# Compressed-branch logits: keys held in the array and queries streamed, instead of queries held and keys streamed

## Chip, cores and metric

One core of one Trainium2 chip runs one program. The metric is the time of one execution on the device in microseconds (us). The kernel is a float32 kernel: products that need the accuracy are made from a high and a low part of each operand, each part in a 4-byte format that TensorE streams in one pass (`F32R` in the code).

## The reference, cut to what matters

Two layers of a decoder trunk on 512 tokens of 1024 channels. Layer 0 mixes tokens with a short convolution, layer 1 with sparse attention; each layer has a half-step SwiGLU feed-forward before and after its mixer. The change touches one of the attention's three branches, the compressed one. 16 heads stand in 4 groups of 4, the head dimension is 64, and each group has 31 compressed keys:

```python
dist_c = t[:, None] - cmp_end[None, :]
s_c = (jnp.einsum('bghqd,bgnd->bghqn', qb, k_cmp).astype(f32) * scale
       + rb[:, :, t5_bucket(dist_c)])
p_c = masked_softmax(s_c, dist_c >= 0)
o_c = jnp.einsum('bghqn,bgnd->bghqd', p_c.astype(v_cmp.dtype), v_cmp)
```

The selected and the window branch (`o_s`, `o_w`) are ordinary causal attention over 512 keys here, since all 8 blocks of 64 tokens are selected, and `out` is the sum of the three branches, each times a gate.

## The kernel before, in words

The program runs feed-forward, convolution, feed-forward, feed-forward, attention, feed-forward one after the other. A scheduler orders the instructions of each engine when the program is built, by their order in the source, by priorities and by a model of durations; on the chip each engine then takes its own list strictly in that order and waits at an instruction until what it needs is there.

The attention's inner part is `attend`. Its loop over `v` runs through 32 units `(g, q, b)`: group, head in the group, branch (0 and 1 are the two branches over 512 keys). At a step it makes the logits of unit `v + 3` on TensorE (`s`, L1061), adds the bias table `tb` and takes the extremum on VectorE (L1071), takes exponentials on ScalarE (L1080), scales them on GpSimd (`L`, L1091), turns those of unit `v + 1` by transposes (`pt`, L1100, then `pth` on ScalarE and `ptl` on VectorE), and applies those of unit `v` to the values (`o`, L1117 and L1118). Other work is put between: projections of the next group's queries (`nat`), turning of queries and keys (`pq` and `pk` in `turners`), the output projection of a finished group (`y`, then `yt` on ScalarE and an addition to `x` on GpSimd), and loads of weights (`wraw`, `whi`, `wlo`, `ehhi`, `ehlo`).

`compressed(g)` is the compressed branch of one group, cut by `yield` into pieces that the loop runs at steps `8g - 2`, `8g - 1` (two) and `8g`. For group 0 these stand at the start of the loop. The logits go into one PSUM tile `pc` (tag `nat`): columns are query block `i` (4), head `q` (4) and key `n` (32 with the pad). `Q[q]` holds a head's 512 queries in 128 rows: the high part in one half of the rows and the low part in the other. `kch` and `kcl` hold the keys' high and low parts, repeated in both halves, so two products per tile give all four part products. After that VectorE adds the bias (`lc`, L1022), takes the minimum (`mc`) and subtracts (`pcs`), ScalarE takes exponentials, VectorE normalises, four transposes (`pct`, L1041) turn the weights, and `finish` applies them with `vz` to the sum `o` of a head.

PSUM has four tags of two tiles each: `nat`, `s`, `t`, `o`. The tag `nat` serves the projections `nat`, the turned keys and queries, `pc`, `pct` and `y`; an instruction that starts a tile waits until the readers of the tile that had the place before are done. The SBUF tag `sq` has two tiles as well and serves the squares of a projection and `yt`.

Of the kernel before, what the change touches and what calls it, by code (L numbers as in the profile page):

```python
# [13 lines left out]
F32 = mybir.dt.float32  # L14
F32R = mybir.dt.float32r
I32 = mybir.dt.int32
AF = mybir.ActivationFunctionType
# [5 lines left out]
P = 128  # L23
# [10 lines left out]
HD = 64  # L34
NHEAD = 16
NG = 4
NCMP = 31
NPAD = 32
# [15 lines left out]
def decoder_kernel(ctx, tc, xT, cT, ng, adaw, adab, ffi, ffo, cwi, cw, cwo,  # L54
                   nwi, nwg, pos, w1, w2, qg, kg, nwo, rb, onehot, rowok, out):
    nc = tc.nc

    def pool(es, name, bufs, **kw):
        kw.setdefault("reuse_waits", "tile")
        return es.enter_context(tc.tile_pool(name=name, bufs=bufs, **kw))  # L60
# [16 lines left out]
    def psum(name, tag="mm"):  # L77
        tag = next(six) if tag == "mm" else {"pr": "o"}.get(tag, tag)
        return ps.tile([P, T], F32, name=name, tag=tag, bufs=2)
# [4 lines left out]
    def tmp(name, n=T, tag="t"):  # L84
        bufs, size = TAGS[tag]
        return tp.tile([P, n], F32, name=name, tag=tag, padded_shape=[P, size], bufs=bufs)
# [3 lines left out]
    ap = ada_es.enter_context(tc.tile_pool(name="ada", bufs=4))  # L90
# [13 lines left out]
    ident = cst.tile([P, P], F32, name="ident")  # L104
# [64 lines left out]
    def split(src, hi, lo):  # L169
        nc.scalar.activation(hi, src, AF.Copy)  # L170
        nc.vector.tensor_tensor(lo, src, hi, ALU.subtract)  # L171
# [535 lines left out]
    def nsa(s, nrm, nxt, w0, ahead):  # L707
        with ExitStack() as es:
# [112 lines left out]
            with ExitStack() as es2:  # L821
# [31 lines left out]
                run(v1[1:])  # L853
                keys(0, 1)
            return attend(es, s, nxt, ahead, K, Q, keys, heads, vn, kch, kcl, vcc, gsb, query_steps, value_steps, last_weight, hpool)


# [126 lines left out]
    def attend(nsa_es, s, nxt, ahead, K, Q, keys, heads, vn, kch, kcl, vcc, gsb, query_steps, value_steps, last_weight, hpool):  # L984
# [3 lines left out]
        with ExitStack() as es:  # L988
            at = pool(es, "at", 1)
# [3 lines left out]
            pcs = at.tile([P, NB, NG, NPAD], F32, name="pcs")  # L993
            vz = at.tile([P, NG, P], F32R, name="vz")
            nc.gpsimd.memset(vz.bitcast(F32), 0.0)

            def table(g, q):
                n = g * NG + q
                for e in range(P // NR):
                    src = bass.AP(tensor=tbl.tensor, offset=tbl.offset + n * NR * TBL + P - 1 - NR * e,  # L1000
                                  ap=[[TBL - 1, NR], [1, T]])
                    nc.sync.dma_start(tb[NR * e:NR * (e + 1), q, :], src)
# [4 lines left out]
            fl = lambda a: a.rearrange("p i q n -> p (i q) n")  # L1007

            def compressed(g):
                pc = psum("pc", "nat")  # L1010
                gc = slice(g * NPAD, (g + 1) * NPAD)
                for i in range(NB):
                    for q in range(NG):
                        oc = pc[:, (i * NG + q) * NPAD:(i * NG + q + 1) * NPAD]
                        for n, m in enumerate((kch, kcl)):
                            nc.tensor.matmul(oc, Q[q][:, i * P:(i + 1) * P], m[:, gc], start=(n == 0), stop=(n == 1))
                    if i == 1:
                        yield
                pv = pc.rearrange("p (i q n) -> p i q n", i=NB, q=NG)
                for i in range(NB):  # L1020
                    nb, c0 = 8 * i + 7, 415 - 128 * i
                    nc.vector.tensor_tensor(lc[:, i, :, 0:nb], pv[:, i, :, 0:nb],  # L1022
                                            tb[:, :, c0:c0 + 16 * (nb - 1) + 1:16], ALU.add)
                mc = sp.tile([P, 16], F32, name="mc", bufs=2)
                nc.vector.tensor_reduce(mc, fl(lc), axis=AX.X, op=ALU.min)
                nc.vector.tensor_tensor(fl(pcs), fl(lc), mc[:, :, None].to_broadcast([P, 16, NPAD]), ALU.subtract)
                nc.scalar.activation(pcs, pcs, AF.Exp, scale=-1.0)
                yield
                sc = sp.tile([P, 16], F32, name="sc", bufs=2)
                nc.vector.tensor_reduce(sc, fl(pcs)[:, :, 0:NCMP], axis=AX.X, op=ALU.add)  # L1030
                fc = sp.tile([P, NB, NG], F32, name="fc", bufs=2)
                nc.vector.reciprocal(fc.rearrange("p i q -> p (i q)"), sc)
                gv = gsb[:, :, g * 12:(g + 1) * 12].rearrange("p i (q r) -> p i q r", r=3)
                nc.vector.tensor_tensor(fc, fc, gv[:, :, :, 0], ALU.mult)
                nc.vector.tensor_scalar(fc[:, 0, :], fc[:, 0, :], rowm, None, op0=ALU.mult)
                nc.vector.tensor_tensor(fl(pcs), fl(pcs), fc.rearrange("p i q -> p (i q)")[:, :, None].to_broadcast([P, 16, NPAD]),
                                        ALU.mult)
                yield
                pt = psum("pct", "nat")
                for i in range(NB):  # L1040
                    nc.tensor.transpose(pt[:, i * P:(i + 1) * P], pcs[:, i].rearrange("p q n -> p (q n)"), ident)  # L1041
                split(pt, pch, pcl)
                for q in range(NG):
                    nc.gpsimd.tensor_copy(vz[q * NPAD:q * NPAD + NCMP, q, :],
                                          vcc[g * NPAD:g * NPAD + NCMP].rearrange("p a b -> p (a b)"))
                yield
# [113 lines left out]
            for g in range(NG):  # L1160
                v0 = 8 * g
                c = compressed(g)
                for q in range(NG):
                    tables[max(v0 - 9 + 2 * q, START)].append((g, q))
                if g:
                    needed[v0 - 5].append(lambda g=g: heads(g, 0))
                    needed[v0 - 4].append(lambda g=g: keys(g, 0))
                    needed[v0 - 3].append(lambda g=g: keys(g, 1))
                    needed[v0 - 2].append(lambda g=g: heads(g, 1))
                for v in (v0 - 2, v0 - 1, v0 - 1, v0):  # L1170
                    needed[v].append(lambda c=c: next(c))
# [7 lines left out]
            def share(v):  # L1179
                for steps, v0, v1 in shares:  # L1180
                    if v0 <= v < v1:
                        n = 11
                        return steps, n * (v - v0 + 1) // (v1 - v0) - n * (v - v0) // (v1 - v0), v == v1 - 1
                return None, 0, False

            for v in range(START, N):
                a, b, u = v + LEAD, v + 1, v
                steps, n, end = share(v)
# [150 lines left out]
```

## Time and profile before

| | |
|---|---|
| three runs | 1966.22, 1966.75, 1969.36 us (median 1966.75) |
| the profiled execution | 1965.66 us, of which the profile's span is 1963.9 us |
| TensorE matmuls (PE) busy | 1914.6 us in 12680 matmuls |
| VectorE (DVE), ScalarE (ACT), GpSimd (POOL) busy | 1455.6, 879.6, 208.7 us |
| granted TensorE clock, mean over the span | 0.995 |
| the loop of `attend` | about 1364.5 to 1600 us of the span |

In rows of the timeline the columns are start in us, time in us, engine, line, operation, `output<-inputs`, the stationary operand's rows*columns and the shape that is streamed, and how often; in square brackets the idle time before it and what ended it. Matmuls overlap in the pipeline, so their cost is read from start to start. In a row of stretches each engine has its busy time and its number of instructions, then come the granted clock (PEclk), the share of the DMA engines and their GB/s. In rows of groups the busy time and the mean duration in ns stand behind the count.

### The profile page before, as it was taken

To read this page: it belongs to the slowest core of one execution; us is meant where nothing else is said; L and a number is where in the kernel's file an instruction comes from. 1 tells how busy PE (TensorE), PEld (TensorE's weight loads), DVE (VectorE), ACT (ScalarE), POOL (GpSimd) and SP (SyncE) were. 2 spreads that over 40 slices of the span, in tenths; PEclk is the share of its full clock that TensorE was granted. 3 is DMA by queue.
4 is the path that set the end of the run, shared out by engine and by line. 5 is a ranking of instruction groups with operands and counts; after the bars stand their busy time and mean duration, and the time that the engine had idled before them with its cause. 6 is when DMAs were issued, how large, how long until landed. Compare 5 with 4: busy or idle time off the path is not lost.

```text
span 1963.9 us, 32479 instructions
## 1 busy us (share of the span) xinstructions
PE 1914.6 (97%) x12680; PEld 1741.9 (89%) x12680; DVE 1455.6 (74%) x2557; ACT 879.6 (45%) x1417; POOL 208.7 (11%) x292
## 2 busy tenths in 40 slices
PE   5999999999999999999999999999999899999999
PEld 3878888898899898999989899999889789898989
DVE  7888889674467586878858687885786878686865
ACT  3322222242236353434635343466787956353532
POOL 0000000100010000000000000002444630010000
PEclk9999999999999999999999999999999999999999
DMA  8898999522245564533556453146322533765621
GB/s 305 303 329 303 333 317 329 195 97 97 76 118 163 144 177 140 149 125 104 168 138 178 140 150 123 52 140 156 83 60 60 128 78 100 192 172 143 172 81 65
DMA packets 113670, 313.42 MB, mean 160 GB/s; under 512 B 13995, under 2 KB 14267, under 8 KB 113516
## 3 DMA queue, kind: packets, MB, share of 16 engines
q1 hardware_dynamic: 96300, 274.02, 41.1%
q0 software_dynamic: 17216, 37.33, 11.2%
q8 instruction: 99, 1.62, 0.4%
q14 instruction: 55, 0.45, 0.1%
HBM read 308.15 MB, written 3.15 MB: 159 GB/s over the span
## 4 chain that ended last, share of the span: by engine, by line
PE 86%; DVE 6%; ACT 4%; issue 2%; DMA 1%; SPq 0%; DVEq 0%; ACTq 0%
PE gu L181 13%; PE gu L179 13%; PE gu L180 13%; PE y L179 7%; PE y L181 7%; PE y L180 7%; PE hs L180 2%; PE hs L179 2%; PE hs L181 2%; PE cv L179 2%; PE cv L180 2%; PE cv L181 2%; PE ty L180 1%; PE ty L179 1%; PE ty L181 1%
## 5 line engine op out<-in xcount | busy, mean ns | idle before, releaser
L170 ACT ACTIVATE whi<-wraw 128x1024 fp32r<-128x1024 f32 (+2 forms) x274 | 270.8, 996 | 506.1 <-PE y L180 218.0
L171 DVE TENSOR_TENSOR wlo<-wraw,whi 128x1024 fp32r<-128x1024 f32 (+2 forms) x274 | 312.1, 1144 | 57.6 <-ACT whi L170 55.3
L179 PE MATMUL gu<-hhi,whi 128*128 128x256 f32 (+1 forms) x880 | 277.6, 315 | 0.0
L181 PE MATMUL gu<-hhi,wlo 128*128 128x256 f32 (+1 forms) x880 | 277.5, 315 | 0.0
L180 PE MATMUL gu<-hlo,whi 128*128 128x256 f32 (+1 forms) x880 | 277.5, 315 | 0.0
L179 PE MATMUL y<-ahi,whi 128*128 128x512 f32 x587 | 228.6, 389 | 0.0
L180 PE MATMUL y<-alo,whi 128*128 128x512 f32 x587 | 228.5, 389 | 0.0
L181 PE MATMUL y<-ahi,wlo 128*128 128x512 f32 x587 | 228.3, 389 | 0.0
L125 DVE CUSTOM_DVE_ANT_0 adaraw<-adaraw,cond 128x1024 f32<-128x1024 f32 x144 | 174.6, 1222 | 38.7 <-DMA adaraw<-in_adaw 36.7
L180 PEld LDWEIGHTS gu<-hlo,whi 128*128 128x128 f32 x880 | 165.1, 188 | 12.2
L179 PEld LDWEIGHTS gu<-hhi,whi 128*128 128x128 f32 x880 | 165.2, 188 | 12.0
L181 PEld LDWEIGHTS gu<-hhi,wlo 128*128 128x128 f32 x880 | 165.2, 188 | 11.9
L516 POOL DMA_DIRECT2D qa<-in_ffi x54 | 65.0, 1204 | 795.0 <-DVE wlo L171 299.2
L179 PEld LDWEIGHTS y<-ahi,whi 128*128 128x128 f32 x587 | 110.2, 188 | 23.3 <-issue 0.8
L181 PEld LDWEIGHTS y<-ahi,wlo 128*128 128x128 f32 x587 | 110.2, 188 | 23.1
L180 PEld LDWEIGHTS y<-alo,whi 128*128 128x128 f32 x587 | 110.2, 188 | 22.5
L592 DVE SCALAR_TENSOR_TENSOR x<-y,mods,x 128x512 f32<-128x512 f32 x72 | 53.4, 750 | 95.2 <-PE y L181 95.1
L179 PE MATMUL gu<-th,qbh 128*128 128x256 f32 x432 | 119.6, 277 | 1.1 <-ACT qbh L170 1.0
L181 PE MATMUL gu<-th,qbl 128*128 128x256 f32 x432 | 119.6, 277 | 0.7 <-DVE qbl L171 0.7
L180 PE MATMUL gu<-tl,qbh 128*128 128x256 f32 x432 | 119.3, 276 | 0.0
L179 PE MATMUL gu<-th,qah 128*128 128x256 f32 x432 | 119.2, 276 | 0.0
L180 PE MATMUL gu<-tl,qah 128*128 128x256 f32 x432 | 119.2, 276 | 0.0
(308 smaller groups left out, 5142.8 us busy)
## 6 DMA issues: line engine op xcount, KB each, us to landing
adaraw<-in_adaw SPq DMA_DIRECT2D x144, 512.0 KB, 6.0
wraw<-in_ffi SPq DMA_DIRECT2D x122, 512.0 KB, 4.0
qa<-in_ffi SPq DMA_DIRECT2D x108, 256.0 KB, 3.8
qa<-in_ffi POOLq DMA_DIRECT2D x54, 512.0 KB, 6.5
wraw<-in_ffo SPq DMA_DIRECT2D x72, 384.0 KB, 4.1
a<-in_ffi SPq DMA_DIRECT2D x54, 256.0 KB, 5.1
wraw<-in_cwi SPq DMA_DIRECT2D x24, 512.0 KB, 3.3
wraw<-in_nwi SPq DMA_DIRECT2D x20, 512.0 KB, 4.2
```

The source lines that it names most:

```text
L125: nc.vector.tensor_tensor_reduce(out=raw, in0=raw, in1=cond, scale=1.0, scalar=0.0, op0=ALU.mult, op1=ALU.add, accum_out=m)
L170: nc.scalar.activation(hi, src, AF.Copy)
L171: nc.vector.tensor_tensor(lo, src, hi, ALU.subtract)
L179: nc.tensor.matmul(o, sh, mh, start=first, stop=False)
L180: nc.tensor.matmul(o, sh, ml, start=False, stop=False)
L181: nc.tensor.matmul(o, sl, mh, start=False, stop=last)
L516: nc.gpsimd.dma_start(qa, bass.AP(tensor=a21.tensor, offset=a21.offset, ap=[a21.ap[0], [0, 2], a21.ap[1]]), accum_op=ALU.add)
L592: lambda d, o: nc.vector.scalar_tensor_tensor(x[d], o, mod(s, 2, d), x[d], op0=ALU.mult, op1=ALU.add))
```

## The change

The logits of a group are made with the keys as the stationary operand. Two new tiles `kz[0]` and `kz[1]` of 128x128 hold zeros; for a group, GpSimd copies its 32 key columns (high parts into one, low parts into the other) to columns 0 to 31 and once more to columns 96 to 127. Columns 0 to 63 then put a head's 32 logits into rows 0 to 31 of the output, columns 64 to 127 put them into rows 32 to 63, with zeros in the other rows. Two heads, each with two products, accumulate into one `pk` tile of 64 rows by 512 queries; ScalarE copies it into half of the rows of an SBUF tile `kq`. After both pairs of heads, four transposes of 128x128 turn `kq` into `pc`, in the layout that it had. The `yield` that stood amid the products stands ahead of the transposes.

```diff
             nc.gpsimd.memset(vz.bitcast(F32), 0.0)
+            kz = [at.tile([P, P], F32R, name=f"kz{e}") for e in range(2)]
+            for z in kz:
+                nc.gpsimd.memset(z.bitcast(F32), 0.0)
...
             def compressed(g):
+                for z, m in zip(kz, (kch, kcl)):
+                    diag = bass.AP(tensor=z.tensor, offset=z.offset, ap=[z.ap[0], [HD + NPAD, 2], [1, NPAD]])
+                    nc.gpsimd.tensor_copy(diag, m[:, None, g * NPAD:(g + 1) * NPAD].to_broadcast([P, 2, NPAD]))
+                kq = tmp("kq", tag="sq")
+                for e in range(2):
+                    pk = psum("pk", "nat")
+                    for n, (q, z) in enumerate((q, z) for q in range(2) for z in kz):
+                        nc.tensor.matmul(pk[0:HD], z[:, q * HD:(q + 1) * HD], Q[2 * e + q], start=(n == 0), stop=(n == 3))
+                    nc.scalar.activation(kq[e * HD:(e + 1) * HD], pk[0:HD], AF.Copy)
+                yield
                 pc = psum("pc", "nat")
-                gc = slice(g * NPAD, (g + 1) * NPAD)
                 for i in range(NB):
-                    for q in range(NG):
-                        oc = pc[:, (i * NG + q) * NPAD:(i * NG + q + 1) * NPAD]
-                        for n, m in enumerate((kch, kcl)):
-                            nc.tensor.matmul(oc, Q[q][:, i * P:(i + 1) * P], m[:, gc], start=(n == 0), stop=(n == 1))
-                    if i == 1:
-                        yield
+                    nc.tensor.transpose(pc[:, i * P:(i + 1) * P], kq[:, i * P:(i + 1) * P], ident)
```

Below the change the lines move by 7 (L1061 becomes L1068, L1100 becomes L1107). What the scheduler makes of it is seen in the lists. On TensorE at group 0, between the logits of the second unit and the first projection, before:

```order
L1061 MATMUL s<-k_12311,q_12312 128x128
L179 MATMUL nat<-whi,hhi_12284 128x256
...
L181 MATMUL nat<-whi,hlo_12289 128x256
L1061 MATMUL s<-k_12308,q_12313 128x512
L1061 MATMUL s<-k_12309,q_12313 128x512
L1100 MATMUL pt<-ident,L 128x128 x4
L1016 MATMUL pc<-kch,q_12312 128x32
```

and after:

```order
L1020 MATMUL pk<-q_12315,kz_13508 64x512
...
L1068 MATMUL s<-k_12311,q_12312 128x256
L1107 MATMUL pt<-ident,L 128x128 x5
L179 MATMUL nat<-whi,hhi_12284 128x256
...
L1068 MATMUL s<-k_12309,q_12313 128x512
L1107 MATMUL pt<-ident,L 128x128
L1025 MATMUL pc<-ident,kq 128x128 x4
```

The first turns `pt`, which need the scaled `L` of the first unit, stand ahead of the twelve projection matmuls now and stood behind them before. On TensorE at group 2, where two of the heads (`q_12314`, `q_12315`) become ready late, before (the rows left out are further `pc`):

```order
L956 MATMUL pq<-ident,qn_14355 128x128 x2
L1016 MATMUL pc<-kch,q_12312 128x32
...
L1061 MATMUL s<-k_12309,q_12313 128x512
L1100 MATMUL pt<-ident,L 128x128 x4
...
L1118 MATMUL o<-ptl_15387,vn_12301 128x384
L1117 MATMUL o<-pth_15386,vn_12303 128x128
L1118 MATMUL o<-ptl_15387,vn_12303 128x128
L1061 MATMUL s<-k_12308,q_12313 128x384
```

and after, from the second pair of heads on:

```order
L1020 MATMUL pk<-q_12314,kz_13508 64x512
L1068 MATMUL s<-k_12310,q_12312 128x256
L1068 MATMUL s<-k_12311,q_12312 128x256
L1107 MATMUL pt<-ident,L 128x128
L1020 MATMUL pk<-q_12315,kz_13507 64x512
...
L1068 MATMUL s<-k_12309,q_12313 128x512
L1107 MATMUL pt<-ident,L 128x128 x4
L1025 MATMUL pc<-ident,kq 128x128 x4
L1124 MATMUL o<-pth_15362,vn_12301 128x384
```

Logits `s` of 256 columns stand behind products of the late heads now, and the transposes into `pc` follow directly on the turns `pt`. On ScalarE at group 3, before:

```order
L1080 ACTIVATE L,st<-L,st 128x512
L975 ACTIVATE q_12314<-pq,qgs 64x512
L975 ACTIVATE q_12315<-pq,qgs 64x512
L1104 ACTIVATE pth_16204<-pt 128x512
...
L176 ACTIVATE ehhi<-wraw 128x1024
L174 ACTIVATE ehlo<-wraw 128x1024
```

and after:

```order
L176 ACTIVATE ehhi<-wraw 128x1024
L1087 ACTIVATE L,st<-L,st 128x512
L975 ACTIVATE q_12314<-pq,qgs 64x512
L975 ACTIVATE q_12315<-pq,qgs 64x512
L1111 ACTIVATE pth_16169<-pt 128x512
...
L174 ACTIVATE ehlo<-wraw 128x1024
L1021 ACTIVATE kq<-pk 64x512
L1158 ACTIVATE yt<-y,mods 128x512
...
L1021 ACTIVATE kq<-pk 64x512
```

The two copies `kq` stand behind a weight copy `ehlo`, with one `yt` between them, and the copy `ehhi` moved ahead of the heads. The lists of the engines are the same up to the loop of `attend`, and after it but for the order of a few rows; the queue of SP is unchanged.

## Prediction, made before the changed kernel was run

> **What bounds the kernel now.** I read the page first, for the span, the engines and the chain of work that ended last.
>
> ```profile
> span 1963.9 us, 32479 instructions
> PE 1914.6 (97%) x12680; PEld 1741.9 (89%) x12680; DVE 1455.6 (74%) x2557; ACT 879.6 (45%) x1417; POOL 208.7 (11%) x292
> PE 86%; DVE 6%; ACT 4%; issue 2%; DMA 1%; SPq 0%; DVEq 0%; ACTq 0%
> ```
>
> The chain lies on TensorE for 86% of the span. The mean of a whole program hides the stage that is edited, so next I cut the loop of `attend` into four stretches, one around each group's compressed logits.
>
> ```profile
> 1364.50:1426.70 62.20, 58.20 (x416) 52.51 (x415) 45.92 (x146) 50.34 (x125) 25.88 (x54) 0.97 0.42 100
> 1426.70:1484.10 57.40, 54.48 (x352) 48.39 (x351) 44.15 (x128) 48.57 (x116) 31.76 (x53) 0.97 0.33 74
> 1484.10:1547.50 63.40, 59.23 (x398) 53.41 (x396) 47.69 (x143) 52.02 (x126) 29.52 (x55) 0.95 0.43 92
> 1547.50:1600.00 52.50, 49.44 (x322) 42.08 (x319) 41.31 (x112) 43.97 (x105) 30.24 (x47) 1.00 0.25 74
> sum 235.50, PE 221.35 PEld 196.39 DVE 179.08 ACT 194.90 POOL 117.40; mean PE 55.34 PEld 49.10 DVE 44.77 ACT 48.73 POOL 29.35
> ```
>
> Here ACT is busy for 194.90 of 235.50 us, far from its 45% of the program, and DVE for 179.08. TensorE leads with 221.35, but the stage is a pipeline of three loaded engines, and work that goes from PE to ACT isn't free by itself. The clock is below 1 in three stretches. Two views answer what the products cost: the groups of instructions by form, and the timeline.
>
> ```profile
> L1016 PE MATMUL pc<-kcl,q 128*128 128x32 f32 x64 | 15.8, 274 | 0.0
> L1016 PE MATMUL pc<-kch,q 128*128 128x32 f32 x64 | 15.8, 274 | 1.1 <-DVE q L977 1.0
> L956 PE MATMUL pk<-ident,kn 128*64 128x128 f32 x32 | 5.4, 272 | 0.3 <-DVE q L977 0.3
> L1132 ACT ACTIVATE osum<-o 64x512 f32<-64x512 f32 x16 | 9.5, 593 | 2.7 <-PE o L1126 2.3
> ...
> 1434.04 0.26 PE L1016 MATMUL pc<-kch,q 128*128 128x32 f32 x1
> 1435.83 0.42 PE L1117 MATMUL o<-pth,vn 128*128 128x384 f32 x1
> ...
> 1552.15 0.40 PE L181 MATMUL y<-ohi,wlo 128*128 128x512 f32 x1
> 1552.38 0.39 PE L179 MATMUL y<-ohi,whi 128*128 128x512 f32 x1
> ```
>
> Sixteen `pc` products stand between 1434.04 and the `o` at 1435.83, so one costs 1.79 / 16 = 0.112 us from start to start though it streams 32 columns; each loads 128 stationary columns. A product with 512 columns costs 0.23 us. The last view is the clock, window by window of 3.41 us.
>
> ```profile
> 1422.98:1426.39 3.41, 3.41 (x31) 3.41 (x30) 2.26 (x6) 3.00 (x6) 1.81 (x4) 1.00 0.00 0
> 1426.39:1429.80 3.41, 2.81 (x26) 2.63 (x24) 2.56 (x7) 2.31 (x7) 0.00 (x0) 1.00 0.00 0
> 1429.80:1433.21 3.41, 3.41 (x16) 3.23 (x15) 1.02 (x4) 0.87 (x3) 1.84 (x5) 0.50 0.00 0
> 1364.94:1368.36 3.42, 3.22 (x25) 3.03 (x25) 2.49 (x10) 3.42 (x11) 1.33 (x2) 1.00 0.77 131
> 1368.36:1371.77 3.41, 3.41 (x16) 3.32 (x16) 1.97 (x9) 2.77 (x12) 1.18 (x4) 0.50 1.06 221
> 1487.82:1491.24 3.42, 2.78 (x21) 2.55 (x21) 2.71 (x9) 2.72 (x9) 0.00 (x0) 1.00 0.76 205
> 1491.24:1498.07 6.83, 6.83 (x33) 6.83 (x32) 4.24 (x15) 2.01 (x5) 2.26 (x5) 0.50 0.10 19
> ```
>
> At groups 0, 1 and 2 a window with a burst of `pc` is followed by one (at group 2 by two) at a granted clock of 0.50, which gets through 16 matmuls where a full one has 31. The burst windows were at least 81% busy (2.78 of 3.42), but with narrow products. I read this as: narrow streaming pulls the clock down for the next window.
>
> **The change, part by part.** *Removed:* 32 products a group, 32 x 0.112 = 3.58 us. *Added on TensorE:* eight products of 512 columns, 8 x 0.23 = 1.84 us, and four transposes. No row has a 64-column stationary with 512 columns streamed; more than the 0.23 of the 128-column one is excluded by nothing, less is not expected since 512 columns pass. Four turns of 128 columns have these rows:
>
> ```profile
> 1422.64 0.60 PE L1100 MATMUL pt<-ident,L 128*128 128x128 f32 x4
> 1423.08 0.60 PE L956 MATMUL pq<-ident,qn 128*128 128x128 f32 x4
> 1423.43 0.42 PE L1117 MATMUL o<-pth,vn 128*128 128x384 f32 x1
> ...
> 1475.49 0.60 PE L1100 MATMUL pt<-ident,L 128*128 128x128 f32 x4
> 1475.93 0.60 PE L956 MATMUL pk<-ident,kn 128*64 128x128 f32 x4
> 1476.29 0.48 PE L179 MATMUL y<-ohi,whi 128*128 128x512 f32 x1
> ```
>
> Four cost 0.44 or 0.35 us; I take 0.44. So a group goes from 3.58 to 2.28 us on PE: 1.3 us less, 5.2 us over four groups.
>
> *The clock.* A halved window loses half of 3.41 us at most, 1.7; by the counts of matmuls (16 against 31, wider ones among the 16) I take 1.5 us each. Four of them are 6.1 us, and I expect them to go, since 512 columns at 0.23 us stream without a break. Bounds: 0 (they stay) and 6.8.
>
> *Added on ACT:* eight copies `kq` of 64x512. The nearest row is `osum`, the same shape out of PSUM, 593 ns: 8 x 0.59 = 4.7 us. *Added on POOL:* two zeroings and eight small copies into `kz`; POOL is busy 117.40 of 235.50 us, and they need only that the products of the group before are done, a whole group earlier; nothing. DMAs and SP's queue have no edit.
>
> *New hand-offs.* `pc` took one place of tag `nat` once; now `pk`, `pk`, `pc` follow each other through a tag of two, of which a projection often holds one. TensorE then stands for PE → ACT (0.59) → PE, up to twice a group. Behind the waiting product are queued all later `s`, `pt` and `o`, so DVE and ACT starve next. Here each group has its own rows.
>
> ```profile
> 1370.15 0.17 DVE L1086 RECIPROCAL r<-st 128x4 f32<-128x4 f32 x1
> 1370.78 2.06 POOL L1091 TENSOR_SCALAR L<-L,f 128x128 f32<-128x128 f32 x4
> 1374.81 0.77 PE L1061 MATMUL s<-k,q 128*128 128x384 f32 x4
> 1434.38 0.60 ACT L1104 ACTIVATE pth<-pt 128x512 fp32r<-128x512 f32 x1 [3.40 <-PE pt L1100]
> 1487.13 1.53 DVE L977 SCALAR_TENSOR_TENSOR q<-pq,qgs,q 64x512 fp32r<-64x512 f32 x2 [0.63 <-ACT q L975]
> 1495.12 1.27 PE L1061 MATMUL s<-k,q 128*128 128x384 f32 x4
> 1497.36 0.60 ACT L1104 ACTIVATE pth<-pt 128x512 fp32r<-128x512 f32 x1 [4.65 <-PE pt L1100]
> 1551.70 1.05 ACT L174 ACTIVATE ehlo<-wraw 128x1024 fp32r<-128x1024 f32 x1
> 1556.60 0.36 PE L1117 MATMUL o<-pth,vn 128*128 128x256 f32 x1
> 1564.14 0.66 PE L1041 MATMUL pct<-ident,pcs 128*128 128x128 f32 x4 [0.94 <-DVE pcs L1036]
> ```
>
> - Group 0 (counted to the `s` at 1374.81): +1.3 and +1.5 for its window. But `pt` now stands ahead of the twelve projection products, and its input is the scaled `L`: DVE's `r` at 1370.15, then 2.06 us on POOL, ends at 1372.84. TensorE would come to `pt` near 1369 (an estimate: the burst ended within the window up to 1368.36, and `s` follows it); I put the `L` 1.2 us earlier than before (`r` moves up one place and all before it shortens), at 1371.6. Of these 2.6 us I count 0.4 as a wait that stood there before too: −2.2. Sum +0.6.
> - Group 1 (to the `o` at 1435.83): +1.3 +1.5. The second `pk`, the projection and `pc` wait for readers on ACT: a bit more than a copy and a half of 0.59, −1.0. ACT's idle time of 3.40 us covers its copies. Sum +1.8.
> - Group 2 (to the `s` at 1495.12): +1.3, and two windows +3.1. The late heads' `q` (DVE, 1487.13 to 1488.66) now hold up only the second `pk`, with `s` and turns between: +0.4. The copies lie in ACT's idle 4.65 us. Sum +4.8.
> - Group 3 (to the `o` at 1556.60): +1.3, no window. `kq` stands behind `ehlo`, which ends at 1552.75, so the first copy ends near 1553.3, the second after `yt` near 1555.6: −1.15. `lc` then comes later, and `pct` at 1564.14 already waited 0.94 us for DVE's chain: −0.55. Sum −0.4.
>
> Together 0.6 + 1.8 + 4.8 − 0.4 = 6.8 us by landmarks. How much reaches the end? In a stage where PE is busy 94% of the time (221.35 / 235.50) most of it does, but between groups ACT (83%) and DVE (76%) wait least; bounds are 0 and all, I take three quarters: 5.1 us. The profiled execution's own time is 1965.66 us, so 1960.5. The median of the three runs, 1966.75, is 1.1 above it: 1961.6, rounded 1961.5.
>
> **Two rules of the skill against the rows.** First a price for the new shapes. Going from a 128-column to a 64-column stationary shows none here: `pt` to `pk` (128*64) takes 0.44 us like `pt` to `pq`, and `pk` to the product behind it 0.36 against 0.35. The Trainium skill, "TensorEngine Tiling (Array Packing)", Key Properties, says that changing the tiling mode drains TensorE. Taken at its word, each of the 20 or so switches that the new `pk` bring would add a drain of about 0.39 − 0.23 = 0.16 us (an estimate from the `y` rows' duration and spacing), 3.2 us in all. The rows above bear it out not at all, so the sum goes without it.
>
> Second the clock. The row is a clock of 0.50 after windows in which TensorE stood for 0.64 us at most (3.42 − 2.78). The Trainium skill, "TensorE: Matmul & The Clock Gate", Part 1 and "HAM oscillation — how this bites in real kernels", gives a free-running window of 3413 ns and two clocks, full and half, as here; its rule that only idle gaps over some 3.4 us throttle would not tie the halving to narrow products. By that rule the windows' 6.1 us need not go.
>
> **The rivals.**
> - *Gains eaten by the hand-offs.* TensorE's 5.2 us and the windows are there, but the waits at `pk` and `pc` and the stand at group 0 are paid in full: two copies and their wake-ups, 1.4 us a group, cancel the 1.3, and half clock comes back at group 0 because TensorE stands 2.5 us in a window. Left are two or three windows, and ACT and DVE between the groups set the pace: 1965 to 1966.5. For it: ACT at 83%; against: its idle 3.40 and 4.65 us lie just there.
> - *Everything is carried through.* 5.2 + 6.1 = 11.3 us less: 1955.5. Against it: `L` at group 0 and `ehlo` at group 3 are seen to be late.
> - *The edit doesn't do what it says:* halved windows stay, or a switch costs 0.16 us. Then 5.1 − 0.75 x 6.1 = 0.5 us of gain is left, or 5.1 − 3.2 = 1.9: 1964.5 to 1966.
> - *Slower: ACT becomes the bound.* Eight copies of 0.59, 4.7 us, stand in ACT's strict order ahead of exponentials for which DVE and PE wait. If PE's wait for `kq` passes 1.3 us in every group, and windows stay halved since PE now stands, the 4.7 us go onto the path: 1966.75 + 4.7 = 1971.5. It decides wherever `kq` stands behind long ACT work, as at group 3. Against it: the idle rows at 1434.38 and 1497.36.
>
> **Numbers.** Forecast 0.44 with its own range of 1957 to 1964; hand-offs 0.25; all carried 0.12; no effect of the clock, or drains 0.07; slower 0.12. About 0.2%, 3.9 us, is what a measurement of this kernel can tell from no change: faster is below 1962.8, slower above 1970.7. Faster: nearly all of the forecast (0.38) and the full carry (0.12), 0.50. Same: the rest of the forecast, hand-offs and no effect, 0.06 + 0.25 + 0.07 = 0.38. Slower 0.12. The range of 1955 to 1969.5 leaves out half of the full carry and most of the slower case, under 2 in 10.
>
> **What would show it.** Eight `pk` products 0.23 us apart and four transposes in 0.44 us; no row at clock 0.50 in the windows behind groups 1 and 2 (a stretch row near 1.00 instead of 0.97 and 0.95); `kq` at 0.59 us; at group 0 a wait of TensorE at `pt` for POOL's `L`, 2 to 2.6 us; at group 3 a wait for `kq` behind `ehlo`. The forecast is wrong if `pk` products stand over 0.3 us apart, if half clock stays, or if the groups after the landmarks take longer than before by what was gained.

## The result, and the profile after

The changed kernel took 1957.47 us (median of six runs, 1955.17 to 1959.34) against 1967.63 us before (six runs, 1965.95 to 1970.82): a ratio of 0.9948 with a 95% interval of 0.9938 to 0.9958. Timed once more later, it was 0.9955 (0.9942 to 0.9967). The prediction was 1961.5 with a range of 1955 to 1969.5, and faster. The time fell by 10.2 us, twice the 5.1 that the forecast took off.

The page of the changed kernel, span, engines and chain:

```profile
span 1953.4 us, 32342 instructions
PE 1902.4 (97%) x12600; PEld 1725.7 (88%) x12600; DVE 1456.4 (75%) x2557; ACT 883.6 (45%) x1425; POOL 211.6 (11%) x302
PE 85%; DVE 7%; ACT 4%; issue 2%; DMA 1%; SPq 0%; POOL 0%; DVEq 0%; ACTq 0%
```

There are 80 matmuls fewer (128 products replaced by 32 products and 16 transposes), and PE is busy 12.2 us less. The page doesn't say where. The loop of `attend` cut at the same four places (the stretches start where the same instructions do) does:

```profile
1361.60:1421.89 60.29, 56.59 (x397) 48.80 (x395) 45.81 (x147) 51.10 (x127) 26.84 (x56) 1.00 0.42 105
1421.89:1477.38 55.49, 51.92 (x332) 44.78 (x331) 44.07 (x128) 49.89 (x118) 32.48 (x55) 1.00 0.35 77
1477.38:1537.31 59.93, 54.48 (x378) 48.37 (x376) 47.17 (x143) 53.52 (x126) 30.17 (x57) 1.00 0.44 98
1537.31:1589.79 52.48, 48.49 (x302) 40.16 (x299) 42.37 (x112) 44.81 (x108) 30.13 (x47) 1.00 0.27 78
sum 228.19, PE 211.48 PEld 182.11 DVE 179.42 ACT 199.32 POOL 119.63; mean PE 52.87 PEld 45.53 DVE 44.86 ACT 49.83 POOL 29.91
```

The first three are 1.9, 1.9 and 3.5 us shorter, the fourth is the same (7.3 in all; the table further down starts some ten us earlier and has 7.7), and PEclk is 1.00 everywhere. PE is busy 9.9 us less (221.35 to 211.48) and stands longer than before: 228.19 − 211.48 = 16.7 us against 14.2. That doesn't part the two causes yet, since both half clock and the removed products make up busy time. The windows of 3.41 us around groups 0, 1 and 2:

```profile
1363.52:1366.93 3.41, 3.19 (x16) 1.86 (x13) 2.50 (x11) 3.41 (x13) 1.54 (x5) 1.00 0.92 191
1366.93:1370.35 3.42, 2.85 (x19) 2.37 (x20) 0.83 (x7) 3.37 (x9) 2.49 (x6) 1.00 1.01 225
1421.55:1424.96 3.41, 2.79 (x17) 1.88 (x16) 2.54 (x8) 2.40 (x8) 0.00 (x0) 1.00 0.00 0
1424.96:1428.37 3.41, 3.36 (x25) 2.76 (x24) 1.76 (x5) 2.81 (x7) 2.65 (x7) 1.00 0.01 2
1479.57:1482.99 3.42, 2.47 (x17) 1.91 (x17) 2.52 (x7) 3.34 (x6) 1.77 (x5) 1.00 0.64 115
1482.99:1486.40 3.41, 3.41 (x27) 3.23 (x26) 3.09 (x12) 3.36 (x12) 0.90 (x4) 1.00 0.46 159
```

The window at 1479.57 has PE busy for only 2.47 us in 17 matmuls, less than the burst windows before (2.78 and 2.81), and the window behind it runs at full clock. So it isn't how long PE is busy that decides. What differs is what was streamed: matmuls with some 4700 columns start in this window, with some 2400 and 2100 in those two. The new instructions by form, and three places in the timeline:

```profile
L1020 PE MATMUL pk<-q,kz 128*64 128x512 f32 x32 | 9.4, 406 | 1.9 <-DVE q L977 1.6 <-ACT kq L1021 0.3
L1021 ACT ACTIVATE kq<-pk 64x512 f32<-64x512 f32 x8 | 4.7, 588 | 0.6 <-PE pk L1020 0.4
L1025 PE MATMUL pc<-ident,kq 128*128 128x128 f32 x16 | 2.5, 276 | 0.0
...
1366.83 2.06 POOL L1098 TENSOR_SCALAR L<-L,f 128x128 f32<-128x128 f32 x4
1367.25 1.46 PE L1107 MATMUL pt<-ident,L 128*128 128x128 f32 x5 [0.54 <-POOL L L1098]
1368.47 0.36 PE L179 MATMUL nat<-whi,hhi 128*128 128x256 f32 x1
...
1428.14 0.60 PE L1025 MATMUL pc<-ident,kq 128*128 128x128 f32 x4
1428.50 0.42 PE L1124 MATMUL o<-pth,vn 128*128 128x384 f32 x1
...
1481.30 0.66 PE L1020 MATMUL pk<-q,kz 128*64 128x512 f32 x2 [0.95 <-DVE q L977]
...
1540.73 1.12 PE L1020 MATMUL pk<-q,kz 128*64 128x512 f32 x4
1541.68 0.60 PE L1107 MATMUL pt<-ident,L 128*128 128x128 f32 x4
1542.38 0.58 ACT L1021 ACTIVATE kq<-pk 64x512 f32<-64x512 f32 x1
1543.01 1.14 PE L1020 MATMUL pk<-q,kz 128*64 128x512 f32 x4 [0.25 <-ACT kq L1021]
1544.75 0.59 ACT L1021 ACTIVATE kq<-pk 64x512 f32<-64x512 f32 x1
1545.39 0.66 PE L1025 MATMUL pc<-ident,kq 128*128 128x128 f32 x4
```

Four `pk` products take 0.95 us (1540.73 to 1541.68), 0.24 each with the switch to 128 columns behind them, and four transposes 0.36 us (1428.14 to 1428.50).

### The profile page after: what moved, and what is told of

It is laid out like the page before. It is cut to its first block, busy times and chain, and to the rows that moved or that the text cites. A ratio compares the mean times of both kernels' runs of the same rounds, so it can differ in the third digit from the quotient of the medians.

```text
span 1953.4 us, 32342 instructions
## 1 busy us (share of the span) xinstructions
PE 1902.4 (97%) x12600; PEld 1725.7 (88%) x12600; DVE 1456.4 (75%) x2557; ACT 883.6 (45%) x1425; POOL 211.6 (11%) x302
## 4 chain that ended last, share of the span: by engine, by line
PE 85%; DVE 7%; ACT 4%; issue 2%; DMA 1%; SPq 0%; POOL 0%; DVEq 0%; ACTq 0%
PE gu L181 13%; PE gu L180 13%; PE gu L179 13%; PE y L179 7%; PE y L180 7%; PE y L181 7%; PE hs L180 2%; PE hs L179 2%; PE hs L181 2%; PE cv L179 2%; PE cv L181 2%; PE cv L180 2%; PE ty L180 2%; PE ty L179 1%; PE ty L181 1%
## 5 line engine op out<-in xcount | busy, mean ns | idle before, releaser
L180 PEld LDWEIGHTS gu<-hlo,whi 128*128 128x128 f32 x880 | 165.1, 188 | 12.2
```

Of the source, the lines that this page charges most:

```text
L180: nc.tensor.matmul(o, sh, ml, start=False, stop=False)
```

## How the traces are compared

A landmark is an instruction of ACT, DVE, POOL or SP with the same operands and shape, the n-th of its kind in both traces. How much earlier than in the trace of before it starts is its gain; the median over a quiet stretch ahead of the loop, between the groups and behind it gives the gain up to there, and the differences are what each group gained. "Ahead" is what a trace had gained before the loop, where the programs are the same.

| trace | ahead | group 0 | 1 | 2 | 3 | loop | halved windows in the loop |
|---|---|---|---|---|---|---|---|
| before, second | −0.8 | −0.1 | −0.1 | −0.1 | 0.0 | −0.2 | 4, the same places |
| before, third | −1.0 | 0.4 | −0.1 | 0.0 | 0.1 | 0.4 | 4, the same places |
| changed | 2.5 | 2.3 | 1.9 | 3.5 | 0.0 | 7.7 | 0 |
| changed, second | −1.1 | 2.3 | 1.9 | 3.4 | 0.1 | 7.7 | 0 |
| changed, third | 2.0 | 2.3 | 1.9 | 3.4 | 0.1 | 7.6 | 0 |
| before, 128 columns | 2.5 | 3.6 | 1.9 | 2.7 | −2.2 | 6.0 | 1, group 3 |
| before, 64 columns | −1.0 | 2.9 | 1.9 | 3.1 | 0.7 | 8.6 | 0 |
| before, 64, second | 0.9 | 3.2 | 1.9 | −1.6 | 0.7 | 4.1 | 3, group 2 |
| changed, products doubled | −1.6 | 3.0 | 0.7 | 1.8 | −2.0 | 3.5 | 1, group 3 |
| changed, copies doubled | 1.0 | 2.1 | 1.9 | 2.7 | −1.5 | 5.3 | 1, group 3 |
| one accumulator | 1.0 | 4.0 | 2.1 | 3.5 | 0.7 | 10.2 | 0 |
| one accumulator, second | −0.8 | 3.4 | 2.0 | 3.7 | 0.7 | 9.7 | 0 |
| one accumulator, DVE copy | −2.9 | 3.2 | 2.2 | 3.8 | 0.1 | 9.3 | 0 |

So of the 10.5 us between the first two traces 2.5 lay ahead of the loop, in code that is the same; there the traces differ by −2.9 to +2.5 whatever the kernel. Of the 2.5 us, 1.6 are one halved window near 921 us, which the first trace of before has and the changed kernel's has not. The change is worth 7.7 us in the loop, three times alike.

## Experiments

**Is the half clock a property of the program?** The kernel before, twice, and the changed one, once, traced again without an edit.

> The kernel before, unchanged, for another trace of the same program: the windows of 3.41 us may fall elsewhere on the loop. Theory (a window with few streamed columns halves the clock of the next): three to five halved windows in the loop again, each right behind a window in which the matmuls' columns fill under about 0.38 of the full rate, and most of them behind the pc bursts; the loop's length follows their number at about 2 us each. Rival (they were chance in the one trace): none or one in the loop, with the length of the loop the same.

> The kernel before, unchanged, once more, with the same expectations as the second trace; where the grid of windows falls differently, the number of halved windows in the loop may differ, and the loop's length with it.

> The changed kernel, unchanged, for a second trace. Theory: no halved window at groups 0 to 2, the loop within 0.5 us of the first trace there; at group 3, where doubled products and doubled copies had one, one halved window is possible by the grid and costs about 2 us. Rival (the first trace was a lucky one): halved windows at groups 0 to 2 as before the change.

They took 1967.53, 1966.70 and 1958.04 us. The same four windows were halved in all three traces of before (at 1369, 1431 and, two long, 1492), none in the loop of the changed one. But the grid of windows stood almost alike in the three: a window ends 0.4, 0.4 and 0.8 us behind the start of the loop's first logits, where the traces of the changed kernel have 1.9, 3.4 and 3.1. So these traces by themselves leave open that the place of the grid spared the changed kernel, and the number of windows in the loop didn't vary with which its length could have been compared.

The granted clocks of all the runs settle it. They average 0.9949 over 42 runs of the kernel before (0.992 to 0.997) and 0.9982 over 12 of the changed one. A halved window loses half of 3.41 us, so that is 5.9 and 2.1 halved windows a run over the whole program: 3.8 fewer, on average over many runs. Among the 42 runs the time does follow the clock, at about 1.0 us a halved window (standard error 0.14) rather than the 2 us expected, windows outside the loop included.

**The clock, with the products kept.** The 128 narrow products stay, with their loads and spacing, but each streams its 32 key columns four times, or twice; the extra columns fall on blocks that are written afterwards.

```diff
-    nc.tensor.matmul(oc, Q[q][:, i * P:(i + 1) * P], m[:, gc], start=(n == 0), stop=(n == 1))
+    w = min(4, 16 - i * NG - q)              # 2 in the 64-column kernel
+    ow4 = pc[:, (i * NG + q) * NPAD:(i * NG + q + w) * NPAD].rearrange("p (r n) -> p r n", r=w)
+    nc.tensor.matmul(ow4, Q[q][:, i * P:(i + 1) * P], m[:, None, gc].to_broadcast([P, w, NPAD]),
+                     start=(n == 0), stop=(n == 1))
```

> The kernel before with the same 128 narrow products, but each streams the 32 key columns four times (128 columns; the extra ones land in places that the next block overwrites), so loads, their spacing and all other work stay. Theory (narrow streaming halves the clock of the next window): no window at clock 0.50 behind groups 0, 1 and 2, products still 0.11 us apart, the loop of attend 4 to 6 us shorter than before, 1961 to 1963 us. Rival (the windows are halved for another cause, an idle gap or chance): half clock stays in the loop, time as before within 1.5 us.

> The kernel before with each narrow product streaming its 32 key columns twice (64 columns), half the dose of the four-fold one. Theory (a window's streamed columns decide): sixteen products add 16 x 32 columns, about 0.06 of a window's full rate; group 0's window (0.375 before) stays at full clock, those of groups 1 and 2 (0.22 to 0.29) come to 0.28 to 0.35, where both was seen, so one to three halved windows are left. Rival (the number of loads or the burst itself decides): four halved windows as before.

> The kernel before with 64 streamed columns in place of 32, timed. Theory (the clock alone makes the gain, the saved loads nothing that the hand-offs don't take back): the loop 8 to 9 us shorter than before, the time 0.995 to 0.997 of before, no worse than the changed kernel by more than 2 us. Rival (the saved loads carry half of the gain): 0.997 or more, 3 to 5 us slower than the changed kernel.

Four times: 1961.32 us (1958.88 to 1964.32), ratio 0.9962 (0.9947 to 0.9976). Twice: 1959.80 us in one run, then 1960.92 (1959.37 to 1962.85), ratio 0.9963 (0.9949 to 0.9976). The products still start 0.11 us apart, with 64 columns and with 128. Streaming more for nothing saves 7 us. The granted clock of the 12 runs averages 0.9971: 2.6 halved windows a run fewer than before, not all of the 3.8. With 64 columns, group 1's two windows, and below them three of the second trace:

```profile
1423.20:1426.61 3.41, 2.81 (x25) 2.63 (x24) 2.94 (x6) 3.16 (x8) 0.00 (x0) 1.00 0.00 0
1426.61:1430.02 3.41, 3.41 (x27) 3.18 (x27) 1.09 (x5) 0.87 (x3) 1.01 (x4) 1.00 0.00 0
```

```profile
1480.89:1484.30 3.41, 2.48 (x19) 1.95 (x17) 2.98 (x8) 3.36 (x9) 0.92 (x2) 1.00 0.86 187
1484.30:1494.54 10.24, 10.24 (x47) 9.95 (x47) 5.56 (x17) 3.78 (x11) 2.27 (x5) 0.50 0.17 49
```

The first row has the same busy time as the burst window of before (2.81 us, 25 matmuls where 26 stood), but full clock follows. The wider products aren't the whole difference: the grid lies otherwise, 12 of the 16 products fall into this window, and it streams some 3500 columns where that of before had some 2100. One to three halved windows in the loop were expected. The first trace of the 64-column kernel had none and a loop 8.6 us shorter, 0.9 more than the change gets with 80 matmuls fewer. In its second trace the loop was only 4.1 us shorter, where 8 to 9 were expected: three windows of group 2 were halved, and that group lost 3.1 + 1.6 = 4.7 us against the first, 1.56 us a window, from two executions of one program. A second price stands ahead of the loop, where all fourteen traces run the same code. Five of them have a halved window near 921 us and nine have none; across it (from 850 to 915 us to 935 to 1000 us) each of the nine gains 1.58 or 1.59 us on the first trace of before, which has the window, and the other four gain 0.0 to 0.1.

Sixty-four columns stand on the edge, and the kernels with wider products end behind the changed one: ratios of 0.9962 and 0.9963 against 0.9948 and 0.9955, 1.4 to 3 us. A reserve: the scheduler counts a wider product as longer and put some logits elsewhere, at group 0 above all, so 2.9 to 3.6 us there aren't the clock's alone; and behind the loop these kernels gave back 0.7 to 1.8 us near 1660 to 1700, which I did not trace to a cause.

**TensorE's time, doubled.** Each `pk` product gets a second one against the zero columns of `kz`.

```diff
-    nc.tensor.matmul(pk[0:HD], z[:, q * HD:(q + 1) * HD], Q[2 * e + q], start=(n == 0), stop=(n == 3))
+    nc.tensor.matmul(pk[0:HD], kz[0][:, NPAD:P - NPAD], Q[2 * e + q], start=(n == 0), stop=False)
+    nc.tensor.matmul(pk[0:HD], z[:, q * HD:(q + 1) * HD], Q[2 * e + q], start=False, stop=(n == 3))
```

> The changed kernel with every pk product doubled by one against a stationary of zeros (the sum stays): 8 x 0.23 = 1.84 us more on TensorE a group, 7.4 us in all, no other engine touched. Theory (TensorE sets the pace of the loop, what it gains or loses arrives in whole): 6.5 to 8 us slower than the changed kernel. The prediction's three quarters: 5.5 us. Rival (ACT and DVE set the pace between groups): 0 to 2.5 us.

1961.86 us (1960.81 to 1964.86), ratio to before 0.9968 (0.9956 to 0.9980). By its trace the loop lost 7.7 − 3.5 = 4.2 us of 7.4 added, but two other things are in that. A window at 1559.6 was halved, which belongs to this trace: over its seven runs the granted clock averages 0.9981, much as with the changed kernel (0.9982). And at group 0 this kernel is 0.7 us ahead of the changed one, though it does more there, since the scheduler put the first turns `pt` behind the twelve projection products again and the wait for `L` is gone. Groups 1 to 3 lost 1.2, 1.7 and 2.0 us of 1.84 each; with 1.56 us off for the window, 3.3 of 5.5 us arrived, some 60%. My theory that TensorE's time arrives in whole fell. The prediction's three quarters can't be told from 60% here: against the changed kernel the ratios differ by 0.0013 to 0.0020, 2.6 to 3.9 us, with intervals of 2.4 us either way.

**ACT's copies, doubled.**

```diff
-    nc.scalar.activation(kq[e * HD:(e + 1) * HD], pk[0:HD], AF.Copy)
+    for _ in range(2):
+        nc.scalar.activation(kq[e * HD:(e + 1) * HD], pk[0:HD], AF.Copy)
```

> The changed kernel with each copy kq made twice on ACT: 8 x 0.59 = 4.7 us more there. Theory (the copies lie beside TensorE's work): 0 to 1.5 us slower than the changed kernel, most of it at group 3, where kq is late already. Rival (ACT is the bound or nearly so): 4 to 5 us slower.

1961.77 us (1958.53 to 1962.75), ratio to before 0.9964 (0.9949 to 0.9978). By its trace the loop lost 2.4 us, between the two expectations: 0.2, 0.0 and 0.8 at groups 0 to 2, and 1.5 at group 3, where a window was halved. Its rows:

```profile
1551.77:1555.18 3.41, 2.06 (x15) 1.63 (x13) 3.35 (x5) 3.36 (x7) 1.28 (x1) 1.00 0.00 0
1555.18:1558.60 3.42, 1.91 (x8) 1.07 (x8) 3.42 (x14) 2.92 (x7) 2.27 (x5) 1.00 0.48 153
1558.60:1562.01 3.41, 3.41 (x14) 3.10 (x14) 3.11 (x10) 2.50 (x8) 0.76 (x1) 0.50 0.00 0
```

In the second row no product is narrow; TensorE waits, with eight matmuls and some 2700 columns in the window, and half clock follows as it did behind the narrow bursts. Against ACT as the bound (4 to 5 us) speak groups 0 to 2, where 3.5 us more of copies cost 1.0. Of the rest a good part is the clock: over the six runs it averages 0.9968 against 0.9982, some 1.6 halved windows a run more.

**One hand-off less.** All four heads go into one accumulator of 128 rows, with one copy of 128x512 (0.59 us, like one of 64x512) and one place of `nat` less; eight products as before.

```diff
-    kz = [at.tile([P, P], F32R, name=f"kz{e}") for e in range(2)]
+    kz = at.tile([P, 9 * NPAD], F32R, name="kz")      # keys' high parts in block 3, low parts in block 7
...
+    pk = psum("pk", "nat")
+    for q in range(NG):
+        for c, w in ((3, 4), (7, (1, 2, 4, 4)[q])):
+            nc.tensor.matmul(pk[0:w * NPAD], kz[:, (c - q) * NPAD:(c - q + w) * NPAD], Q[q],
+                             start=(q == 0 and c == 3), stop=(q == 3 and c == 7))
+    nc.scalar.activation(kq, pk, AF.Copy)             # nc.vector.tensor_copy(kq, pk) in the DVE variant
```

> The changed kernel with all four heads in one accumulator of 128 rows: the same eight products, one copy of 128x512 a group (about 0.63 us) instead of two of 0.59, and one place of tag nat less. Theory (hand-offs cost little after the change: 2.7 us of idle time on TensorE's side ends at a kq): 0 to 2 us faster than the changed kernel. Rival (the hand-offs and ACT's copies eat much of the gain): 3 us or more faster.

> One accumulator for all four heads, with its copy kq on VectorE instead of ScalarE (0.6 us a group either way). Theory (what is left of the hand-off is the wait behind ACT's weight copies at group 3): 0 to 1 us faster than one accumulator with the copy on ScalarE. Rival (VectorE's chain of logits and bias is as full): the same or up to 2 us slower.

> The changed kernel, unchanged, timed beside one accumulator on the same chip. Theory: its loop is 7.7 us shorter than before in the trace, as in the two traces so far; 0.995 of the time before.

> One accumulator for all four heads, copy on ScalarE, timed beside the changed kernel on the same chip. Theory (one hand-off of the two is gone): the loop 10 us shorter than before, some 2.5 us under the changed kernel. Rival (its first time was chance): within 1 us of the changed kernel.

1955.52 us (1952.29 to 1957.03), ratio to before 0.9930 (0.9916 to 0.9944); with the copy on DVE 1954.99 (1954.38 to 1958.80), 0.9939 (0.9925 to 0.9952). Beside the changed kernel on one chip: 1956.49 (1954.31 to 1959.51) against 1957.99 (1955.43 to 1960.19), ratios to before 0.9949 (0.9935 to 0.9963) and 0.9955 (0.9942 to 0.9967). The times alone don't part the two; the traces do: loops of 10.2 and 9.7 us gained (9.3 with the copy on DVE) against 7.7, 7.7 and 7.6. This is the best of the kernels by its loop, 2.0 to 2.5 us ahead of the changed kernel with the copy on ScalarE, between the two expectations. Not all of that is the hand-off. At group 0 the first turns stand behind the projection products again, in all three traces of one accumulator, and find `L` nearly ready:

```profile
1367.47 0.28 PE L179 MATMUL nat<-whi,hhi 128*128 128x256 f32 x1
...
1367.83 2.06 POOL L1097 TENSOR_SCALAR L<-L,f 128x128 f32<-128x128 f32 x4
1369.30 0.49 PE L1106 MATMUL pt<-ident,L 128*128 128x128 f32 x3
1369.95 0.33 PE L1106 MATMUL pt<-ident,L 128*128 128x128 f32 x1 [0.16 <-POOL L L1097]
```

So 1.7, 1.1 and 0.9 us of the difference lie at group 0, where order and hand-off can't be told apart. Over groups 1 to 3 one accumulator gains 6.3, 6.4 and 6.1 us against the changed kernel's 5.4: 0.7 to 1.0 us is what the runs show for the hand-offs there. With the copy on VectorE 0 to 1 us more was expected; neither the times nor the loop show it.

## Why the prediction came out, step by step

The direction, the range and most of the places were right. The size came out at half: 5.1 us were taken off, 10.2 measured, and 1957.47 us lies nearer to the rival that carries everything through (1955.5) than to the forecast. That the sum by landmarks, 6.8, comes near the loop's 7.7 is partly luck, since errors of +1.7 and −1.3 us at groups 0 and 2 cancel in it.

- **Prices.** 0.23 us a product and 0.44 for four transposes: measured 0.24 and 0.36. `kq` 0.59: 0.588. From a `pk` to what follows with 128 columns it is 0.23 to 0.24 us in eight of ten places, so no drain shows there (the other two, 0.31 and 0.43, stand at group 0; at the second the kernel before has 0.44 from a `pc` to the same logits). The Trainium skill, "TensorEngine Tiling (Array Packing)", Key Properties, has one at each switch; no run here shows a price for it.
- **The clock**, 1.5 us a window (6.1 for four) and all four gone: 1.56 by two executions of the 64-column kernel and 1.58 ahead of the loop, none left in three traces, and 3.8 windows fewer by the clocks of all runs. This step carried the result: four windows at 1.56 are 6.2 of the loop's 7.7 us. The Trainium skill, "TensorE: Matmul & The Clock Gate", "HAM oscillation — how this bites in real kernels", ties the half clock to idle gaps over some 3.4 us. This trace doesn't agree: a window with 0.60 us of idle time in all (before, 2.81 of 3.41 busy) was followed by it, and one with 0.95 (changed, 2.47 of 3.42) was not. The rival that hung on that rule fell.
- **Group 0**, predicted +0.6: +2.3. I let TensorE wait until the whole `L` was scaled. Each `pt` needs one quarter of it: the first wait was 0.54 us, and five turns took 1.2 us (1367.25 to 1368.47), paced by POOL, instead of 0.55. TensorE's stand was mis-sized at 2.2 us; it was about 1.2. That explains 1.0 of the 1.7 us that the sum is off here; the other 0.7 stays open.
- **Groups 1 and 3**, +1.8 and −0.4: +1.9 and 0.0. At group 3 the copies did come behind `ehlo` and `yt`, at 1542.38 and 1544.75, 2.4 us apart. That they ate the saved 1.3 is argued, not shown: TensorE's one wait for a `kq` in these rows is 0.25 us.
- **Group 2**, +4.8: +3.5. The second `pk` waited 0.95 us for the late heads, where I had counted a gain of 0.4.
- **The share that reaches the end**, three quarters: this step was wrong. All of the 7.7 us were still there at 1650, and 7.9 to 8.6 us at 1900. So 6.8 by landmarks was 0.9 too low, the three quarters took off another 1.7, and the forecast fell short by 2.6 us in the loop. Over the 42 and 12 runs the medians differ by 9.2 us; the 0.6 to 1.3 us beyond that are not placed.
- **The saved products**, 5.2 us: with the hand-offs' −4.0 (−2.2, −1.0, +0.4, −1.15) and the late `lc` of −0.55 I kept 0.7 of them. With four windows at 1.56 off, 1.5 of the loop's 7.7 us are left for the products less their hand-offs: 0.7, 0.3 and 0.4 at groups 0 to 2, nothing at group 3. So most of the 5.2 us didn't pay, as summed. The control can't say it closer: its loop without half clock gained 8.6 us, 2.4 more than four windows, and another order of the logits is in that. The rival "gains eaten by the hand-offs" was nearly right on this term and wrong in letting half clock come back.

Open: the rest of what the traces differ by ahead of the loop (a halved window near 921 us is 1.6 of it), and how much at group 0 is order, in the controls and in one accumulator alike. No kernel changes that order alone.

## What to carry to other kernels

Where TensorE streams few columns for three or four microseconds, look at the granted clock of the next window before counting the products: a cheap burst of narrow matmuls cost about 1.6 us a window here in work that had nothing to do with it, and streaming its columns twice brought 7 us where replacing it brought 9 to 10. Stay clear of the edge rather than at it, as the 64-column kernel's second trace shows. A saving on TensorE in a pipeline of three loaded engines counts only for the part that isn't handed straight to a wait, so count the hand-offs that the new form brings (0.7 to 1.0 us over groups 1 to 3 here). And when a variant gains, see whether the scheduler moved something else: three of the kernels here lost a wait at group 0 in that way.

## What the runs showed of the clock

For each window of the loop I summed the streamed columns of the matmuls that start in it (a typical window has some 5900). Over the fourteen traces, every window of up to 2400 columns was followed by half clock, none over 3072 was, and from 2560 to 3072 both occurred. In the first trace of the 64-column kernel 2880 and 3072 were followed by full clock, in the second 2816 by half; before, 3072 halved at group 0 and did not near 1553. A sum moves by a product, at most 512 columns, when the edge of the window is moved by some hundredths of a us, so these bounds are rough, and they were found on the traces that they describe. How much of the window TensorE was busy didn't order them: one with 2.15 us busy and 2560 columns was followed by full clock, one with 2.81 us and some 2100 by half. In the loop a halved window can also call the next one, since at half clock it streams fewer columns: 832 in the first of the two at group 2.
